# A hybrid streaming encoder layer: state-space and retention products move from GpSimd to VectorE, sampled factors are made first with two load buffers, key weights and the second cache are loaded early

## The chip, the cores and the metric

The kernel runs on one core of one Trainium2 chip. The metric is device time in microseconds of one execution. Five engines work from queues of their own and wait for one another by semaphores: TensorE (PE, whose weight loads are listed as PEld), VectorE (DVE), ScalarE (ACT), GpSimd (POOL) and SyncE (SP). SP computes nothing; it issues nearly all transfers, in the order of its queue.

## The reference

One layer of an encoder on 512 frames of a new stream and on 16 new frames of each of eight running streams: 640 tokens of width 1024. Three mixers read the same normalised projection; their outputs are concatenated and projected back.

```python
def layer(x, pos, ckv_past, krope_past, past_pos, ret_s0, ssm_h0, conv_buf, p):
    x = x + 0.5 * swiglu(rmsnorm(x, p['ffn1_norm']), p['ffn1_wgu'], p['ffn1_wd'])
    cols = rmsnorm(x, p['mix_norm']) @ p['w_in']
    ret_cols, mla_cols, ssm_cols = jnp.split(cols, [RET_COLS, RET_COLS + MLA_COLS], axis=-1)
    o_ret, ret_s = retention_group(...)
    o_mla, c_kv, k_rope = mla_group(...)
    o_ssm, ssm_h, conv_new = ssm_group(...)
    x = x + jnp.concatenate([o_ret, o_mla, o_ssm], axis=-1) @ p['w_out']
    x = x + 0.5 * swiglu(rmsnorm(x, p['ffn2_norm']), p['ffn2_wgu'], p['ffn2_wd'])
```

The running streams bring a cache of 256 latent rows each for the attention (mla_group), and states for retention and for the state-space mixer (ssm_group). The state-space scan, for each chunk and head, is

```python
        xdt = xi * dti[..., None]
        scores = jnp.einsum('bthn,bshn->btsh', ci, bi) * decay
        y = (jnp.einsum('btsh,bshp->bthp', scores, xdt)
             + jnp.einsum('bthn,bhpn->bthp', ci, hs) * jnp.exp(acum)[..., None])
        w = jnp.exp(alast[:, None, :] - acum)
        hs = jnp.exp(alast)[:, :, None, None] * hs + jnp.einsum('bshp,bshn->bhpn', xdt * w[..., None], bi)
```

after which y gets d_skip times x, is gated by silu(z) and normalised.

## The kernel before, in words

Everything is computed in float32. A dense weight or activation is split into a rounded high part and the rest (wh and wl, xh and xl), and each product is three matmuls: high by high, rest by high, high by rest. The high part is an ACT copy (L288), the rest a DVE subtraction (L289). Weights come in pieces of 128x1024 that SP loads.

The stages in the order of time are: FFN1 (to about 450 us), projections for the mixers and attention (450 to 785), convolution and retention (785 to 940), the state-space stage or SSD (940 to 1145), the output projection (to 1190) and FFN2 (to 1628). Code is written in levels of priority (`prio(n)`), and the framework's scheduler orders each engine's queue at build time from these levels and its own estimate of the times; once built, every engine works through a fixed list. So an edit that moves one instruction moves others around it.

What the change touches:

- `spread` (L365) turns a per-token scale into a tile that all partitions hold: two matmuls with a matrix of ones, each copied out of PSUM by ACT (L370). At the start of each FFN, its two halves share one PSUM half (`sb[:, 1]`, L486).
- `wukT`, the key weights of the attention in the latent form, is loaded (L1024) by a transfer that ACT issues just before the matmuls at L1030 use it.
- The sampled attention goes through the eight running streams one by one (`sample_a`, L1140). The cached latents of each are loaded twice, transposed (c_t) and plain (c_n). Stream 0 uses a tile `K` that lies free by then; the others rotate through three buffers.
- The cached rotary keys of all streams (krc) are scaled and rotated by POOL and DVE (L705 to L717).
- Retention multiplies the values by a block mask on POOL (vm, L1370).
- `ssd_a(blk)` (L1530 to L1565) prepares a block of 128 tokens: loads x (yz) and the gate (z), forms xdt = x times dt, xdw = xdt times the decay to the block's end, and yz = x times d_skip, three 128x1024 products on POOL (L1541, L1547, L1548). `ssd_b(blk)` forms the output and the state: yi (L1579) is added to yz on POOL (L1580), the state is scaled and added to on DVE (L1583, L1589), the in-block product on TensorE (L1599) is added (L1600), and the gate is multiplied in (L1601).
- `sample_pre` (L1619 to L1635) makes the factors of the running streams' state update. It loads x of the fifth block into xdw (L1622), scales it on POOL (L1625), splits it (ACT L1628, DVE L1629) and stores the parts to a scratch tensor xw_dr in memory, from which they are read back with the rows of a stream side by side: sr, one load of two transfers for a pair of streams (L1639), with one buffer.
- `sample_step(b)` (L1641) does for stream b and two groups of heads: a load of the state hb, four small matmuls for its output (L1651), hb times the decay on POOL (L1653), the matmul with sr (L1655), the sum on DVE (L1656) and a store.
- `mix_out` (L918) transposes a result into a tile `mo` (two buffers), which SP stores to ma_dr (retention) or ms_dr (SSD). `mix_in` (L1701) loads it back as mraw (three buffers in the first projection) and splits it. `wout` runs the output projection (L1683), first the half with weights woa (retention and attention), whose matmuls also fill the gaps of the SSD stage, then that with weights wos (SSD).
- The gate's projection z (L822) is the other filler; its results are stored through SP to z_dr (L891) and loaded again by `ssd_a` (L1539).

The order of calls is `ssd_a(0)`, `sample_pre()`, and then for each of five blocks: `ssd_a` of the next, two `sample_step`s in each of the first four, `ssd_b`, and `ssd_c` (the transposes) of the one before.

Of the kernel before, what the change touches and what calls it, by code (L numbers as in the profile page):

```python
# [10 lines left out]
F32 = mybir.dt.float32  # L11
# [186 lines left out]
def body(tc, a):  # L198
# [166 lines left out]
    def spread(bank, dg, R):  # L365
        V.tensor_mul(dg.rearrange("p (t c) -> p t c", t=NT), brow(ident, NT), bcol(rstd, P))
        for hf in range(2):
            pr = bank()
            PE.matmul(pr[:, :H2], ones, dg[:, hf * H2:(hf + 1) * H2], start=True, stop=True)
            S.copy(R[:, hf * H2:(hf + 1) * H2], pr[:, :H2])  # L370
# [5 lines left out]
    def xtile(tag, dt=F32):  # L376
        return xt.tile([P, T], dt, tag=tag, name=nm(tag))
# [52 lines left out]
    def ffn(n, tok, first, final, bank, pair, R):  # L430
# [51 lines left out]
        def statistics():  # L482
            with urgent():
                sb = pair()
                norm_stats(lambda: sb[:, 0], G)
                spread(lambda: sb[:, 1], xtile("xl7"), R)  # L486

# [259 lines left out]
    DECB = 5  # L747
    MRAWB = 3
    YZB = 3
# [3 lines left out]
    XWB = 1  # L753
    PRS = 17
    STKB = 1
    SRB = 1
    HBB = 3
# [79 lines left out]
    kf = kvp.tile([P, NC, CR], F32, tag="kf", name="kf")  # L837
    Q.dma_start(out=wukv.rearrange("p a b c -> p (a b c)"), in_=a["wukv"])
    mla_st = ExitStack()
    mp = pool(mla_st, "mlap")  # L840
# [69 lines left out]
    prio(13)  # L910
    spread(one, t0.tile([P, T], F32, tag="sq", name=nm("dg")), R)
    for j, o in ((0, C_QSC), (1, C_KSC)):
# [107 lines left out]
    with ExitStack() as s2:  # L1020
        wk_st = ExitStack()
        wkp = pool(wk_st, "mswk")
        wukT = wkp.tile([64, MH, CKV], F32, tag="wukT", name="wukT")
        nc.scalar.dma_start(out=wukT.rearrange("p h c -> p (h c)"), in_=a["wukT"])  # L1024
        qab = m0.tile([P, 2, DB, MH, DS], F32, tag="qab", name="qab")
# [35 lines left out]
        def prep(u):  # L1061
# [4 lines left out]
            for t in range(4):  # L1066
                pt = one()
                for kv in range(2):
                    for c in range(2):
# [11 lines left out]
                         rs.unsqueeze(3).broadcast_to([P, 4, 4, CR]))  # L1081
            KT = ub.tile([96, 4, SEQ], F32, tag="KT", name=nm("KT"), bufs=2)
            for hh in range(4):
# [51 lines left out]
    with ExitStack() as s2:  # L1135
# [4 lines left out]
        def sample_a(b):  # L1140
            if b == 0:
                kt_ = m0.tile([P, 1600], F32, tag="K", name=nm("K"))
                c_t, c_n = kt_[:, 0:544].rearrange("p (c n) -> p c n", c=2), kt_[:, 544:1056].rearrange("p (c n) -> p c n", c=2)
                iv, krT = kt_[:, 1056:1328], kt_[0:CR, 1328:1600]
            else:
                c_t = t1_.tile([P, 2, 272], F32, tag="c_t", name=nm("c_t"), bufs=3)
                c_n = t1_.tile([P, 2, CKV], F32, tag="c_n", name=nm("c_n"), bufs=3)
                iv = t1_.tile([P, 272], F32, tag="iv", name=nm("iv"))
                krT = t1_.tile([CR, 272], F32, tag="krT", name=nm("krT"))
# [65 lines left out]
    mog_st = ExitStack()  # L1215
    mog = pool(mog_st, "mog", 2)
    ssd_st = ExitStack()
# [115 lines left out]
    def ret_b(blk, rf, vg, qT, at):  # L1333
# [24 lines left out]
        else:  # L1358
            qd = qpad.rearrange("p (b c) -> p b c", c=P + DS)[:, :, 0:DS]
            for r in range(4):  # L1360
# [8 lines left out]
                vm = rb.tile([P, DB, P], F32, tag="vm", name=nm("vm"))  # L1369
                G.tensor_mul(vm, brow(v[:, r * P:(r + 1) * P], DB), bcol(bmask, P))  # L1370
                sc = rb.tile([P, DB, 64], F32, tag="sc", name=nm("sc"))
# [127 lines left out]
    with ExitStack() as s2:  # L1499
# [33 lines left out]
        def ssd_a(blk):  # L1533
# [6 lines left out]
            xdt = big("xdt", XDB)  # L1540
            G.tensor_mul(v16(xdt), v16(yz), bcol(dt[:, blk, :], 64))  # L1541
            bt = xdw = None
            if s == 0:
                bt = sb.tile([P, 256], F32, tag="bt", name=nm("bt"), bufs=BTB)
                trans_b(bt, b0)
                xdw = big("xdw", XWB)
                G.tensor_mul(v16(xdw), v16(xdt), bcol(wl_[:, blk, :], 64))  # L1547
            G.tensor_mul(v16(yz), v16(yz), bcol(rowp[:, R_SSMD:R_SSMD + 16], 64))  # L1548
            pss = bank_a()
# [16 lines left out]
        def ssd_b(blk, bt, xdt, xdw, yz, zt, decs):  # L1566
            s = 1 if blk == 4 else 0
            b0 = blk * P
            for g in range(2):
                gs = slice(g * 512, (g + 1) * 512)  # L1570
                if blk > 0:
# [7 lines left out]
                    V.tensor_mul(v8(yi), v8(pi), bcol(ea[:, blk, 8 * g:8 * g + 8], 64))  # L1579
                    G.tensor_add(yz[:, gs], yz[:, gs], yi)  # L1580
                if s == 0:
# [37 lines left out]
        def sample_pre():  # L1619
            trans_b(bts, SEQ)  # L1620
            xw = big("xdw", XWB)
            Q.dma_start(out=xw, in_=xs_dr[4])  # L1622
            dws = sb.tile([P, SH], F32, tag="dws", name="dws")
            V.tensor_mul(dws, dt[:, 4, :], wl_[:, 4, :])
            G.tensor_mul(v16(xw), v16(xw), bcol(dws, 64))  # L1625
            sh, sl = big("yz", YZB), big("z", ZB)
            bh = sb.tile([P, 256], F32, tag="bh", name="bh")
            S.copy(sh.bitcast(F32R), xw)  # L1628
# [12 lines left out]
        def sample_step(b):  # L1641
# [3 lines left out]
            for g in range(2):  # L1645
# [6 lines left out]
                S.copy(yTs[:, 4 * g:4 * g + 4, b * DS:(b + 1) * DS], pt[:, 0:4 * DS].rearrange("p (c t) -> p c t", c=4))  # L1652
                G.tensor_mul(v8(hb), v8(hb), bcol(els[:, b, 8 * g:8 * g + 8], 64))  # L1653
                pu = bank_s()
                PE.matmul(pu, sr[0][o:o + 48, 1024 + g * P:1024 + (g + 1) * P], sr[0][o:o + 48, gs], start=True, stop=True)  # L1655
                V.tensor_add(hb, hb, pu)  # L1656
                Q.dma_start(out=a["ssms"][b][:, gs], in_=hb)

        cur = ssd_a(0)
        sample_pre()  # L1660
        for blk in range(NT):
            prio(17)
            nxt = ssd_a(blk + 1) if blk + 1 < NT else None
            if blk < 4:
                prio(PRS)
                sample_step(2 * blk)
                sample_step(2 * blk + 1)
                prio(17)
            out = ssd_b(blk, *cur)
# [109 lines left out]
```

## Time and profile before

| | |
|---|---|
| median of 3 runs | 1628.97 us (1628.05 to 1636.07) |
| profiled execution | 1630.27 us, its span 1628.5 us |
| mean granted clock of TensorE | 0.98 |
| TensorE, DVE, ACT, POOL busy | 98%, 69%, 42%, 20% of the span |
| bytes moved | 175.70 MB in 86924 packets |

The span is the time from the first to the last recorded instruction of the profiled execution; the rest of its time lies around it. A line of a group names the source line, the engine, the operation, the tiles (result, then what it reads), the form and the count; then the busy time and the mean of one in ns, and last how long the engine sat idle just ahead and what ended that. A line of the waits says who waited, for which engine's or transfer's result, how long in all, how many times and the longest. In a table by stretches each engine has its busy time (and count of instructions); the granted clock is 1.00 at full speed. The chain is the sequence of work, followed back from the end, in which each step was released by the one before.

### The profile page before, as it was taken

The numbers are of one execution on the slowest core, as the hardware profiler recorded it, in microseconds if no ns is written. First come the engines' busy times: TensorE is split into PE (matmuls) and PEld (weight loads), VectorE is DVE, ScalarE is ACT, GpSimd is POOL, SyncE is SP. The second block draws the span as 40 slices with busy tenths as digits, with TensorE's granted clock in tenths as the row PEclk, the third lists the DMA queues.
The fourth block names the chain that finished last, engine by engine and source line by source line (L and its number), as shares of the span: only waits on it lengthen the run. The fifth ranks groups of instructions, "written<-read, shape, count | busy, mean of one in ns | idle before, by whom it ended". The sixth has DMA issues, their size and how long they took to land.

```text
span 1628.5 us, 27264 instructions
## 1 busy us (share of the span) xinstructions
PE 1592.4 (98%) x10867; PEld 1528.8 (94%) x10867; DVE 1120.2 (69%) x1810; ACT 690.9 (42%) x1270; POOL 332.9 (20%) x361
## 2 busy tenths in 40 slices
PE   9899999999999999999999998999999999999998
PEld 9799999999999999976999887788999999999998
DVE  8878777777575552464799656744779877777762
ACT  7554343334345344553344364423545443433330
POOL 0322222222202000002120134421013222232220
PEclk9999999999999999998999987999999999999999
DMA  5232222222162333213254467764212322222221
GB/s 201 78 104 92 78 78 82 87 78 79 52 205 92 103 111 91 81 53 104 71 180 139 131 188 256 230 188 153 69 46 85 102 80 78 80 90 78 78 78 65
DMA packets 86924, 175.70 MB, mean 108 GB/s; under 512 B 12984, under 2 KB 45144, under 8 KB 86604
## 3 DMA queue, kind: packets, MB, share of 16 engines
q1 hardware_dynamic: 85260, 171.13, 33.2%
q10 hardware_dynamic: 1536, 2.82, 0.6%
q8 instruction: 85, 1.39, 0.4%
q14 instruction: 43, 0.35, 0.1%
HBM read 142.14 MB, written 31.79 MB: 107 GB/s over the span
## 4 chain that ended last, share of the span: by engine, by line
PE 87%; DMA 5%; DVE 4%; ACT 2%; issue 1%; POOL 1%; SPq 0%; ACTq 0%; DVEq 0%; POOLq 0%
PE bank L557 30%; PE pair L600 18%; PE pd L822 11%; PE pd L1683 7%; PE pd L1417 5%; PE pair L464 2%; PE pair L694 1%; PE p L1095 1%; PE po L1117 1%; PE bank L464 1%; PE pb L1599 1%; PE ps L1651 1%; DVE wl L289 1%; DMA xw_dr<-z 1%; DMA sr<-xw_dr 1%
## 5 line engine op out<-in xcount | busy, mean ns | idle before, releaser
L288 ACT CAST wh<-wr 128x1024 fp32r<-128x1024 f32 (+3 forms) x161 | 162.8, 1015 | 174.6 <-PE pair L600 70.7
L289 DVE TENSOR_TENSOR wl<-wr,wh 128x1024 fp32r<-128x1024 f32 (+3 forms) x161 | 198.5, 1234 | 55.6 <-ACT wh L288 50.6
L600 PE MATMUL pair<-xh,wh 128*128 128x320 f32 x672 | 206.6, 309 | 1.1 <-ACT gt L697 0.7
L600 PE MATMUL pair<-xl,wh 128*128 128x320 f32 x672 | 207.4, 309 | 0.0
L600 PE MATMUL pair<-xh,wl 128*128 128x320 f32 x672 | 207.1, 309 | 0.0
L557 PE MATMUL bank<-xsh,wh 128*128 128x320 f32 x656 | 203.0, 310 | 1.6 <-DVE ut L582 1.5
L557 PE MATMUL bank<-xsl,wh 128*128 128x320 f32 x656 | 202.5, 309 | 0.0
L557 PE MATMUL bank<-xsh,wl 128*128 128x320 f32 x656 | 202.5, 309 | 0.0
L524 POOL TENSOR_TENSOR gt<-gt,R 128x320 f32<-128x320 f32 x82 | 93.7, 1143 | 481.5 <-DVE gt L584 427.7
L602 DVE SCALAR_TENSOR_TENSOR x<-pair,x 128x640 f32<-128x640 f32 x96 | 78.7, 822 | 149.9 <-PE pair L600 149.8
L822 PE MATMUL pd<-wh,xh 128*128 128x256 f32 (+1 forms) x560 | 164.2, 293 | 0.1
L822 PE MATMUL pd<-wl,xh 128*128 128x256 f32 (+1 forms) x560 | 163.3, 292 | 0.0
L822 PE MATMUL pd<-wh,xl 128*128 128x256 f32 (+1 forms) x560 | 161.7, 289 | 0.0
L526 POOL TENSOR_TENSOR gt<-gt,R 128x320 f32<-128x320 f32 x82 | 113.8, 1388 | 74.5 <-ACT gt L525 74.5
L600 PEld LDWEIGHTS pair<-xh,wh 128*128 128x128 f32 x672 | 125.8, 188 | 2.1 <-ACT gt L697 1.2
L600 PEld LDWEIGHTS pair<-xl,wh 128*128 128x128 f32 x672 | 126.1, 188 | 0.1
L600 PEld LDWEIGHTS pair<-xh,wl 128*128 128x128 f32 x672 | 126.1, 188 | 0.0
L557 PEld LDWEIGHTS bank<-xsh,wh 128*128 128x128 f32 x656 | 123.3, 188 | 2.9 <-DVE ut L582 2.1
L557 PEld LDWEIGHTS bank<-xsl,wh 128*128 128x128 f32 x656 | 123.3, 188 | 0.3
L557 PEld LDWEIGHTS bank<-xsh,wl 128*128 128x128 f32 x656 | 123.3, 188 | 0.1
L822 PEld LDWEIGHTS pd<-wh,xh 128*128 128x128 f32 x560 | 109.6, 196 | 3.1 <-issue 2.6
L822 PEld LDWEIGHTS pd<-wh,xl 128*128 128x128 f32 x560 | 109.6, 196 | 1.8 <-issue 1.6
(575 smaller groups left out, 4053.9 us busy)
## 6 DMA issues: line engine op xcount, KB each, us to landing
wr<-in_wgu SPq DMA_DIRECT2D x88, 512.0 KB
wr<-in_wd SPq DMA_DIRECT2D x40, 512.0 KB
wr<-in_wint SPq DMA_DIRECT2D x28, 512.0 KB
wr<-in_winx SPq DMA_DIRECT2D x12, 512.0 KB
qk_dr<-stg SPq DMA_DIRECT2D x40, 128.0 KB
wr<-in_woa SPq DMA_DIRECT2D x8, 512.0 KB
hb<-in_sssm SPq DMA_DIRECT2D x16, 256.0 KB
out_ssms<-hb SPq DMA_DIRECT2D x16, 256.0 KB
```

The costliest lines, as they stand in the source:

```text
L288: S.copy(hv, raw)
L289: V.tensor_sub(lv, raw, hv.bitcast(F32))
L464: PE.matmul(out[gu][hf], w_, x_, start=q == 0 and k == 0 and i == 0, stop=q == 3 and k == 1 and i == 2)
L524: G.tensor_mul(gt[:, hf], gt[:, hf], R3[:, hf])
L526: G.tensor_mul(gt[:, hf], gt[:, hf], R3[:, hf])
L557: PE.matmul(out, w_[:, o:o + P], x_[:, PSLOT[p]], start=start and k == 0 and i == 0, stop=k == 3 and i == 2, skip_group_check=not start)
L600: PE.matmul(pt[:, hf, :H2], w_[:, o:o + P], x_[:, hf * H2:(hf + 1) * H2], start=j == 0 and i == 0, stop=j == g - 1 and i == 2)
L602: V.scalar_tensor_tensor(xv, pt[:, :, :H2], 0.5, xv, op0=ALU.mult, op1=ALU.add)
L694: PE.matmul(pt[:, kt], x_[:, o:o + P], w_[cc][:, :512], start=c == 0, stop=c == 5)
L822: PE.matmul(ps[:, :w], x_[k][:, t * P:(t + 1) * P], w_[:, k * w:(k + 1) * w], start=c == 0, stop=c == 23)
L1417: PE.matmul(ps[:, :H2], w_[:, o:o + P], x_[k][:, hf * H2:(hf + 1) * H2], start=c == 0, stop=c == 23)
L1683: PE.matmul(ps[:, :H2], w_[:, o:o + P], x_[k][:, hf * H2:(hf + 1) * H2], start=k == 0 and i == 0, stop=k == NK - 1 and i == 2)
```

## The change

It consists of these edits, all in one diff.

- `spread` takes its two halves from two PSUM halves where it can.
- wukT has a pool of its own, opened at the start of the projections, and is loaded there.
- The tile KT of the first half of the heads is kept in the pool of K; streams 0 and 4 load into K, 1 and 5 into KT, and the other four rotate through two buffers.
- `mo` has one buffer instead of two, mraw two instead of three, sr two instead of one. bh uses a buffer of bt, dws one of qs5.
- The products of `ssd_a`, `ssd_b`, `sample_pre` and `sample_step`, and the masked values vm of retention, are DVE's.
- `sample_pre()` is called ahead of `ssd_a(0)`. The streams of each block are listed in a table, with the same pairs as before.

```diff
@@ spread
-            pr = bank()
+            pr = bank(hf)
...
-                spread(lambda: sb[:, 1], xtile("xl7"), R)
+                spread(lambda hf: sb[:, 1 - hf], xtile("xl7"), R)
...
-    MRAWB = 3
+    MRAWB = 2
...
+    SAMPLED = ((0, 1), (2, 3), (4, 5), (6, 7), ())
...
-    SRB = 1
+    SRB = 2
...
     Q.dma_start(out=wukv.rearrange("p a b c -> p (a b c)"), in_=a["wukv"])
+    wk_st = ExitStack()
+    wkp = pool(wk_st, "mswk", side="right")
+    wukT = wkp.tile([64, MH, CKV], F32, tag="wukT", name="wukT")
+    nc.scalar.dma_start(out=wukT.rearrange("p h c -> p (h c)"), in_=a["wukT"])
...
-            KT = ub.tile([96, 4, SEQ], F32, tag="KT", name=nm("KT"), bufs=2)
+            KT = (ub if u else m0).tile([96, 4, SEQ], F32, tag="KT", name=nm("KT"))
@@ sample_a
-            if b == 0:
-                kt_ = m0.tile([P, 1600], F32, tag="K", name=nm("K"))
+            if b % 4 < 2:
+                kt_ = m0.tile([P, 1600], F32, tag=("K", "KT")[b % 4], name=nm("K"))
...
-                c_t = t1_.tile([P, 2, 272], F32, tag="c_t", name=nm("c_t"), bufs=3)
-                c_n = t1_.tile([P, 2, CKV], F32, tag="c_n", name=nm("c_n"), bufs=3)
+                c_t = t1_.tile([P, 2, 272], F32, tag="c_t", name=nm("c_t"))
+                c_n = t1_.tile([P, 2, CKV], F32, tag="c_n", name=nm("c_n"))
...
-    mog = pool(mog_st, "mog", 2)
+    mog = pool(mog_st, "mog", 1)
...
-                G.tensor_mul(vm, brow(v[:, r * P:(r + 1) * P], DB), bcol(bmask, P))
+                V.tensor_mul(vm, brow(v[:, r * P:(r + 1) * P], DB), bcol(bmask, P))
@@ ssd_a
-            G.tensor_mul(v16(xdt), v16(yz), bcol(dt[:, blk, :], 64))
+            V.tensor_mul(v16(xdt), v16(yz), bcol(dt[:, blk, :], 64))
...
-                G.tensor_mul(v16(xdw), v16(xdt), bcol(wl_[:, blk, :], 64))
-            G.tensor_mul(v16(yz), v16(yz), bcol(rowp[:, R_SSMD:R_SSMD + 16], 64))
+                V.tensor_mul(v16(xdw), v16(xdt), bcol(wl_[:, blk, :], 64))
+            V.tensor_mul(v16(yz), v16(yz), bcol(rowp[:, R_SSMD:R_SSMD + 16], 64))
@@ ssd_b
-                    G.tensor_add(yz[:, gs], yz[:, gs], yi)
+                    V.tensor_add(yz[:, gs], yz[:, gs], yi)
@@ sample_pre
-            dws = sb.tile([P, SH], F32, tag="dws", name="dws")
+            dws = qs5.rearrange("p a t c -> p (a t c)")[:, 0:SH]
...
-            G.tensor_mul(v16(xw), v16(xw), bcol(dws, 64))
+            V.tensor_mul(v16(xw), v16(xw), bcol(dws, 64))
...
-            bh = sb.tile([P, 256], F32, tag="bh", name="bh")
+            bh = sb.tile([P, 256], F32, tag="bt", name="bh", bufs=BTB)
@@ sample_step
-                G.tensor_mul(v8(hb), v8(hb), bcol(els[:, b, 8 * g:8 * g + 8], 64))
+                V.tensor_mul(v8(hb), v8(hb), bcol(els[:, b, 8 * g:8 * g + 8], 64))
@@ the loop over blocks
+        sample_pre()
         cur = ssd_a(0)
-        sample_pre()
...
-            if blk < 4:
-                prio(PRS)
-                sample_step(2 * blk)
-                sample_step(2 * blk + 1)
-                prio(17)
+            prio(PRS)
+            for b in SAMPLED[blk]:
+                sample_step(b)
+            prio(17)
```

How the lists of the engines move is seen at three places. In a row stand the line, the operation, and the tiles written and read; a number behind a name tells tiles of one name apart. The changed file has the same lines up to 5 further down. First SP's queue at the stores of the factors; before:

```order
L1537 DMA yz_10800<-xs_dr_4831 128x1024
L1633 DMA xw_dr<-yz_10785 8x16x1024 x2
L891 DMA z_dr_4820<-stg_10564 128x256
L1539 DMA z_10735<-z_dr_4820 128x1024
L1633 DMA xw_dr<-z_10786 8x16x1024 x2
L1537 DMA yz_10948<-xs_dr_4832 128x1024
L891 DMA z_dr_4821<-stg_10595 128x256
L891 DMA z_dr_4822<-stg_10626 128x256
L1639 DMA sr_10843<-xw_dr 64x1280 x2
L891 DMA z_dr_4823<-stg_10657 128x256
L1539 DMA z_10802<-z_dr_4821 128x1024
```

and after:

```order
L1634 DMA xw_dr<-z_10733 8x16x1024 x2
L896 DMA z_dr_4821<-stg_10419 128x256
L896 DMA z_dr_4822<-stg_10450 128x256
L1705 DMA mraw_11576<-ma_dr 128x320
L896 DMA z_dr_4823<-stg_10481 128x256
L1538 DMA yz_10938<-xs_dr_4832 128x1024
L896 DMA z_dr_4824<-stg_10512 128x256
L1640 DMA sr_10833<-xw_dr 64x1280 x2
L1640 DMA sr_10981<-xw_dr 64x1280 x2
L896 DMA z_dr_4820<-stg_10555 128x256
L896 DMA z_dr_4821<-stg_10586 128x256
L1540 DMA z_10749<-z_dr_4820 128x1024
```

Before, the stores of the factors' low half (read from a z tile) come behind a store and a load of the gate (z_dr, z), and the first load of sr behind two more stores; one load of sr stands there. After, both pairs of sr are loaded ahead of the last two gate stores, and the gate loads of the first blocks follow them.

Then TensorE's queue around the first matmul with sr, before:

```order
L822 MATMUL pd_10662<-wl_10535,xh_644_4767 128x256
L1585 MATMUL pb_11061<-xdw_10811,bt_10806 128x512
L822 MATMUL pd_10662<-wh_10534,xh_653_4788 128x256
L822 MATMUL pd_10662<-wh_10534,xl_654_4789 128x256
L822 MATMUL pd_10662<-wl_10535,xh_653_4788 128x256
L1683 MATMUL pd_11648<-xh_1965_11580,wh_11638 128x320
L1683 MATMUL pd_11648<-xl_1966_11581,wh_11638 128x320
L1683 MATMUL pd_11648<-xh_1965_11580,wl_11639 128x320
L1655 MATMUL ps_10855<-sr_10843 128x512
L1651 MATMUL ps_10861<-bc,hb_10859 128x16 x4
L1599 MATMUL pb_11066<-xdt_10804,dec_10821 128x64 x4
```

and after:

```order
L823 MATMUL pd_10591<-wl_10520,xh_651_4784 128x256
L823 MATMUL pd_10591<-wh_10519,xh_635_4743 128x256
L1575 MATMUL pb_11036<-state_10720,bc 128x512
L1531 MATMUL pa_10945<-ident,bc 128x128 x2
L1656 MATMUL ps_10845<-sr_10833 128x512
L1652 MATMUL ps_10851<-bc,hb_10849 128x16 x4
L823 MATMUL pd_10591<-wh_10519,xl_636_4744 128x256
L823 MATMUL pd_10591<-wl_10520,xh_635_4743 128x256
L823 MATMUL pd_10591<-wh_10525,xh_638_4751 128x256
L823 MATMUL pd_10591<-wh_10525,xl_639_4752 128x256
L823 MATMUL pd_10591<-wl_10526,xh_638_4751 128x256
```

Before, the gate's projection (L822) is at its end when the first L1655 comes, and after it there follow matmuls of the SSD stage and of the output projection (L1683). After, the first L1656 stands among rows of the gate's projection (now L823), of which 62 follow it.

Last DVE's queue in the first block, before:

```order
L890 SCALAR_TENSOR_TENSOR stg_10564<-jnk_10563,stg_10564 128x256
L1579 TENSOR_TENSOR yi_11048<-pb_11046,E 128x512
L1583 TENSOR_TENSOR state_10729<-state_10729,E 128x512
L1562 TENSOR_TENSOR dec_10833<-dec_10833,stm_10817 128x512
L1562 TENSOR_TENSOR dec_10839<-dec_10839,stm_10817 128x512
L1629 TENSOR_TENSOR z_10786<-xdw_10780,yz_10785 128x1024
L890 SCALAR_TENSOR_TENSOR stg_10595<-jnk_10594,stg_10595 128x256
L1553 TENSOR_TENSOR stm_10965<-pa_10962,cst 128x256
L1601 TENSOR_TENSOR yz_10733<-yz_10733,z_10735 128x512 x2
```

and after:

```order
L1580 TENSOR_TENSOR yi_11038<-pb_11036,E 128x512
L1584 TENSOR_TENSOR state_10720<-state_10720,E 128x512
L1549 TENSOR_TENSOR yz_10938<-yz_10938,rowp 128x1024
L1657 TENSOR_TENSOR hb_10836<-hb_10836,ps_10845 128x512
L1654 TENSOR_TENSOR hb_10849<-hb_10849,E 128x512
L1581 TENSOR_TENSOR yz_10790<-yz_10790,yi_11038 128x512
L1554 TENSOR_TENSOR stm_10955<-pa_10952,cst 128x256
L1602 TENSOR_TENSOR yz_10747<-yz_10747,z_10749 128x512 x2
L1590 TENSOR_TENSOR state_10720<-state_10720,pb_11042 128x512
L1580 TENSOR_TENSOR yi_11047<-pb_11045,E 128x512
```

Before, the block's DVE work is decay (L1562), sums and the split of the factors (L1629). After, the POOL products stand among it (L1549, L1654, L1581), the split is gone from this place, and the product with the gate (L1602, which reads z) stands ahead of the state's sum (L1590).

More of the change, by code (lines that the diff above doesn't have):

```diff
@@ L910, in body @@
     prio(13)
-    spread(one, t0.tile([P, T], F32, tag="sq", name=nm("dg")), R)
+    spread(lambda hf: one(), t0.tile([P, T], F32, tag="sq", name=nm("dg")), R)
     for j, o in ((0, C_QSC), (1, C_KSC)):
@@ L1020, in body @@
     with ExitStack() as s2:
[L1021 to L1024, printed above, removed]
         qab = m0.tile([P, 2, DB, MH, DS], F32, tag="qab", name="qab")
```

## The prediction

> **What bounds the kernel now.** I read the page first: busy times, granted clock, the chain.
>
> ```profile
> span 1628.5 us, 27264 instructions
> PE 1592.4 (98%) x10867; PEld 1528.8 (94%) x10867; DVE 1120.2 (69%) x1810; ACT 690.9 (42%) x1270; POOL 332.9 (20%) x361
> PEclk9999999999999999998999987999999999999999
> PE 87%; DMA 5%; DVE 4%; ACT 2%; issue 1%; POOL 1%; SPq 0%; ACTq 0%; DVEq 0%; POOLq 0%
> ```
>
> TensorE sets the time, and nothing in the change takes a matmul of any size away. What can be won is the rest: places where TensorE waits, and the half clock that follows them. A slice of the clock row is 40.7 us; it dips in the 19th (733 to 774 us) and the 24th and 25th (936 to 1018). The next view is the list of TensorE's waits between 440 and 1220 us, where all edits but one lie (us in total, times, longest).
>
> ```profile
> PE ps L1655 <- DMA sr<-xw_dr: 7.0, 2, 4.4
> PE pd L1683 <- ACT xh L1710: 2.1, 2, 1.5
> PE pd L1683 <- DVE xl L1711: 2.1, 2, 1.4
> PE p L1163 <- DMA c_t<-in_ckvT: 1.7, 1, 1.7
> PE px L1030 <- DMA wukT<-in_wukT: 1.4, 1, 1.4
> PE pb L1585 <- DVE state L1589: 0.8, 1, 0.8
> ```
>
> Then a table by stretches; after the busy times of PE, PEld, DVE, ACT and POOL comes the granted clock, then the DMA share.
>
> ```profile
> 600.00:640.00 40.00, 38.58 (x286) 36.84 (x286) 8.05 (x23) 16.40 (x46) 0.52 (x2) 0.91 0.36 99
> 720.00:780.00 60.00, 54.75 (x333) 42.29 (x331) 28.34 (x80) 22.54 (x76) 8.47 (x45) 0.91 0.27 79
> 890.00:940.00 50.00, 49.69 (x390) 45.44 (x389) 34.74 (x92) 20.93 (x40) 7.59 (x4) 1.00 0.50 142
> 940.00:960.00 20.00, 18.77 (x145) 17.28 (x143) 9.05 (x11) 15.07 (x29) 4.93 (x3) 0.96 0.65 200
> 960.00:980.00 20.00, 20.00 (x89) 14.84 (x90) 14.11 (x16) 9.42 (x18) 10.84 (x6) 0.67 0.57 171
> 980.00:1000.00 20.00, 16.26 (x99) 13.27 (x98) 12.80 (x29) 9.34 (x20) 5.33 (x4) 0.93 0.62 178
> 1000.00:1020.00 20.00, 19.34 (x83) 16.89 (x84) 13.06 (x20) 8.72 (x20) 8.51 (x5) 0.59 0.87 324
> 1020.00:1060.00 40.00, 37.83 (x213) 29.60 (x213) 32.17 (x59) 16.25 (x32) 19.45 (x12) 0.96 0.71 234
> 1088.00:1110.00 22.00, 19.42 (x111) 17.65 (x109) 5.54 (x8) 2.85 (x6) 4.18 (x4) 0.84 0.42 130
> 1110.00:1150.00 40.00, 36.53 (x242) 34.61 (x242) 22.60 (x48) 16.35 (x30) 2.56 (x2) 0.96 0.48 151
> ```
>
> A busy TensorE at a clock of 0.67 loses a third of the stretch, and no wait shows it: 20 x 0.33 = 6.6 us in 960 to 980, 20 x 0.41 = 8.2 us in 1000 to 1020. Last the chain of waits through the state-space (SSD) stage, start and length first.
>
> ```profile
> 965.77 5.50 DMA xdw<-xs_dr
> 971.43 1.91 POOL xdw L1625
> 975.70 2.01 DVE stg L890
> 977.73 6.57 DMA z_dr<-stg
> 985.38 10.93 DMA xw_dr<-z
> 996.37 4.25 DMA sr<-xw_dr
> 1089.30 5.38 DMA sr<-xw_dr
> 1133.24 5.48 DMA mraw<-ms_dr
> ```
>
> The first sampled product waits for a train of transfers that begins only at 965.77; SP issues the store of the factors' low half at 985.38, after the z store of 977.73 that stands ahead of it in the queue. The second sr is loaded at 1089.30, because one buffer serves all eight streams.
>
> **Key weights.** The load of wukT moves from just before its use (issued by ACT, TensorE waiting 1.4 us) to the start of the projections. The half clock that follows goes too: 40 x (1 - 0.91) = 3.6 us in 600 to 640, a stretch with no other wait of size. That makes 1.4 + 3.6 = 5.0, and 1.4 if the clock falls anyway.
>
> ```profile
> L1030 PE MATMUL px<-qTs,wukT x32: 271/272/579, 619.7 to 628.9; 64*128 64x128 f32 x32
> ```
>
> The same matmul takes 272 ns or 579 ns within one wait's reach, so a wait of 1.4 us was followed by half speed. [...]
>
> The pools shift as well, and the cached rotary keys are prepared some 35 us earlier: their load and their first POOL product now stand ahead of the last gate product of FFN1.
>
> ```profile
> L710 POOL TENSOR_TENSOR kg_c<-krc x1: 1041/1041/1041, 485.0 to 485.0; 128x512 f32<-128x512 f32 x1
> ```
>
> That product costs FFN1's end between nothing and its 1.0 us plus the load's lateness; with the half clock of the wukT row I bound it by 5, and take 1.
>
> **Sample caches.** Two samples of each four read into buffers that lie free, so their loads run during attention. The 1.7 us at c_t goes; of the 60 x 0.09 = 5.4 us of clock in 720 to 780 some, because several short waits remain. Bounds 0 and 7; I take 3, since the chain from scores to values is as it was.
>
> **First sr.** The load at 965.77 moves ahead of every block's work, and SP reaches the stores of the factors behind weights and not behind z. Their splitting runs on DVE, ACT, DVE without POOL. By the rows above, store and load take 10.9 + 4.3 = 15.2 us; with the stores issued around 961 (DVE frees the last weights by about 959, as now) sr lands near 977. TensorE comes to its first use at about 978, and by the order 62 dense z rows still follow as filler where before none was left. So 4.4 us of wait go, and with them the 8.2 us of clock in 1000 to 1020: 12.6. The clock of 960 to 980 stays, since the dependent chain at the block's start stays. Back comes a wait: the stores and loads of z now stand behind sr on SP. 6.57 us for a z store and 5.5 us for a load of that size from about 974 put z at 986; the gate product that waits for it stands ahead of the next state sum on DVE, and TensorE would want that sum at about 981. I take 5 us, net 12.6 - 5 = 7.6. Bounds: -4 (the wait stays at 4.4 + 4 in another place) and 16 (z no later than needed, and half of the 6.6 us regained).
>
> **Second sr.** With two buffers the load of 1089.30 is issued an early pair ahead. In 1088 to 1110 TensorE idles 22 - 19.42 = 2.6 us and loses 22 x 0.16 = 3.5 us of clock: 6.1, at least 2.6.
>
> **The tail.** The last transposes of y now stand 103 output-projection matmuls ahead of the first that needs them, where 12 stood.
>
> ```profile
> 1128.08 0.31 PE L1683 MATMUL pd<-xh,wl 128*128 128x320 f32 x1
> ...
> 1129.39 0.31 PE L1683 MATMUL pd<-xh,wl 128*128 128x320 f32 x1
> 1131.21 0.57 PE L1683 MATMUL pd<-xh,wh 128*128 128x320 f32 x2 [1.50 <-ACT xh L1710]
> ```
>
> From the first to the second of these rows nine matmuls start in 1.31 us, 146 ns each, so the cover grows from 1.8 to 15 us. The way it must hide runs from the transposes at 1127 to the last xl near 1141, 14 us; the single transpose buffer adds about one store of some 3 us to it (an estimate from half of the 5.48 us load), but the last chunks are used later still. Idle 40 - 36.53 = 3.5 and clock 40 x 0.04 = 1.6 us give 5.1; bounds 2 and 7. The third load buffer that the mixer loses belongs to loads that are far ahead, cost 0, and if that cover is gone one load's 5.48 us in part. The decay vector and the split of b that take another tile's place cost 0: each is read once, ahead of the tile's next owner.
>
> **POOL's products on DVE.** Their rows, and what DVE takes for the like:
>
> ```profile
> L1653 POOL TENSOR_TENSOR hb<-hb,E 128x512 f32<-128x512 f32 x16 | 18.9, 1178 | 54.9 <-PE ps L1651 51.5 <-DVE x L1728 3.4
> L1580 POOL TENSOR_TENSOR yz<-yz,yi 128x512 f32<-128x512 f32 x8 | 11.6, 1446 | 19.1 <-DVE yi L1579 19.0
> L1548 POOL TENSOR_TENSOR yz<-yz,rowp 128x1024 f32<-128x1024 f32 x5 | 10.9, 2174 | 0.2
> L1600 DVE TENSOR_TENSOR yz<-pb,yz 128x512 f32<-128x512 f32 x10 | 6.9, 688 | 9.8 <-PE pb L1599 9.8
> L1629 DVE TENSOR_TENSOR z<-xdw,yz 128x1024 fp32r<-128x1024 f32 x1 | 1.2, 1212 | 0.0
> L289 DVE TENSOR_TENSOR wl<-wr,wh 128x1024 fp32r<-128x1024 f32 x13 | 20.8, 1609 | 5.0 <-ACT wh L288 4.8
> L267 DVE TENSOR_TENSOR rst<-rsy 128x2 f32<-128x2 f32 x15 | 6.2, 416 | 0.3
> ```
>
> 24 half-width products at 0.69 us and 15 full-width ones at 1.21 us are 16.6 + 18.2 = 34.8 us more for DVE between 940 and 1130; four more (vm, 4.8 us) fall in 890 to 940, where DVE has 15 us free and TensorE is not kept waiting. Against that, DVE's own work shortens: the weight split takes 1609 ns here against the 1212 ns of the same shape, 13 x 0.4 = 5.2 us, and a step on two columns takes 416 ns. Each product alone is also quicker, 0.69 for 1.18 to 1.45 us. DVE has 120 - 81.2 = 38.8 us idle between 940 and 1060 (the five rows of the table), so the work fits; but it is a queue, and a product waiting for POOL's old input now holds up what follows. The state waits (0.8 us, and xl's 1.4 in 1020 to 1060) gain up to 3.8 us with their clock (2.2 idle, 1.6 clock), the new order may lose 8; I take a loss of 2.
>
> The second half of the sum of squares in another bank lets the second spreading matmul go ahead of the first copy, at the two FFN starts. One copy less in a chain of several is worth up to 1 us; I cost it at 0.
>
> **Sum.** 5.0 - 1 + 3 + 7.6 + 6.1 + 5.1 - 2 = 23.8 us. The profiled execution took 1630.3 us (span 1628.5 and 1.8 around it), 1.3 above the median of the three runs, 1629.0; so 1606.5 for it, and for the median **1605.2 us**.
>
> **Rivals.**
> *DVE's queue holds half of it.* Between blocks TensorE, ACT and DVE hand one another each step, and sr's wait may be only the last that such a train ends in: then its 12.6 us are not won, and half of the added 34.8 us lies on the path. What is left is the gains outside, 5.0 - 1 + 3 + 6.1 + 5.1 = 18.2, less 17.4: 0.8 us, 1628.2. For it: DVE is busy 32.17 of 40 us in 1020 to 1060, and its new order ties z, state and split together. Against: DVE holds 4% of the chain, and sr's train of transfers starts with a load that nothing of DVE holds back.
> *DVE becomes the bound, slower.* The same, but DVE's 38.8 us of idle time are all such handing over, so that all 34.8 us lengthen the stage: 34.8 - 18.2 = 16.6 us slower, 1645.6. It decides from 18.2 + 8.1 = 26.3 us on the path, three quarters of the added work. Against: much of DVE's idle time waits for TensorE itself (9.8 us before L1600), and POOL, which took longer for the same products, holds 1% of the chain.
> *The clock doesn't come back.* If the short waits that remain keep the clock low, its terms fall: 3.6 for wukT, 2 of the samples' 3, half of sr's 8.2, 3.5 and 1.6, together 14.8; 23.8 - 14.8 = 9.0 are left, 1620.0. The row of L1030 speaks against, and the 1.00 of 890 to 940, where no wait of size stands, speaks for a clock that recovers. [...]
> *More comes.* z is in time and the clock holds from 960 on: 7.6 becomes 16, samples 7, and the loss of 2 goes: 1591.
>
> **How the numbers follow.** Forecast (1597 to 1614) 0.55; more 0.13; clock lost 0.12; half on DVE's queue 0.11; slower 0.09. About 0.5%, 8.1 us, is what a measurement of this kernel can tell from no change, so below 1620.9 counts as faster: the first two and half of the third, 0.74. Within 0.5%: the other half and the fourth, 0.17. Slower: 0.09. The range leaves out the slow rival, the half of the fourth that lies above 1628 and what of "more" lies below 1588, some 0.2 together: 1588 to 1628.
>
> **What would show it.** Right: no wait of px on wukT and L1030 at 272 ns throughout; the sr rows at most 1.5 us of wait in all; a clock over 0.9 in the 20 us after the first sampled product; no ACT or DVE wait at the first matmuls of the second output projection; DVE's weight split near 1.2 us in the SSD stage. Wrong in a term: TensorE waiting for state or yi on DVE for over 5 us, DVE waiting for z. Wrong as a whole: DVE's share of the chain rising from 4% to 6% or more while the stage of 940 to 1150 keeps its 210 us.

## The result, and the profile after

The changed kernel takes 1606.5 us (median of 4 executions, 1604.7 to 1607.7), the kernel before 1629.2: a ratio of 0.985, 95% interval 0.982 to 0.988, 22.8 us faster. The forecast was 1605.2. The profiled execution has a span of 1605.9 us. Its page, in the lines that answer to those shown of before:

```profile
span 1605.9 us, 27198 instructions
PE 1572.9 (98%) x10867; PEld 1515.4 (94%) x10867; DVE 1127.4 (70%) x1853; ACT 693.4 (43%) x1270; POOL 264.8 (16%) x318
PEclk9999999999999999999999988899999999999999
PE 49%; DMA 3%; DVE 1%; ACT 0%; POOL 0%; issue 0%; SPq 0%; DVEq 0%; ACTq 0%; POOLq 0%
```

POOL has lost 43 instructions and 68 us, DVE has gained the 43 and only 7 us. (The chain covers about half of the span this time, so its shares can't be held against those of before.) TensorE's waits between 440 and 1220 us in the changed kernel:

```profile
PE pd L1683 <- ACT xh L1710: 6.8, 2, 6.4
PE ps L1652 <- DMA hb<-in_sssm: 2.6, 1, 2.6
PE pair L600 <- DVE al L381: 2.4, 1, 2.4
PE pa L1559 <- ACT dec L1561: 1.4, 2, 0.7
PE pair L600 <- ACT ah L380: 0.5, 1, 0.5
```

The waits for sr, for wukT, for c_t and for the state are gone. New are one of 6.4 us at the output projection's first operands, one of 2.6 us for the first loaded state, and 2.9 us at the end of FFN1. The table by stretches (busy times of PE, PEld, DVE, ACT, POOL, then clock, DMA share, GB/s):

```profile
600.00:640.00 40.00, 40.00 (x323) 38.49 (x323) 12.43 (x30) 19.37 (x49) 0.53 (x2) 1.00 0.28 89
720.00:780.00 60.00, 55.60 (x372) 44.84 (x372) 31.44 (x95) 22.60 (x74) 8.85 (x46) 1.00 0.24 73
940.00:960.00 20.00, 16.03 (x94) 13.73 (x94) 12.54 (x16) 14.64 (x25) 0.00 (x0) 0.80 0.73 241
960.00:980.00 20.00, 19.27 (x100) 15.04 (x99) 12.49 (x18) 6.58 (x13) 0.00 (x0) 0.76 0.74 226
980.00:1000.00 20.00, 20.00 (x123) 16.02 (x123) 16.42 (x32) 10.57 (x22) 0.00 (x0) 0.93 0.57 190
1000.00:1020.00 20.00, 13.40 (x72) 10.48 (x72) 13.14 (x40) 10.04 (x22) 0.00 (x0) 0.83 1.04 346
1020.00:1060.00 40.00, 39.65 (x227) 32.30 (x226) 34.54 (x64) 15.52 (x30) 0.00 (x0) 0.96 0.75 253
1060.00:1090.00 30.00, 30.00 (x219) 28.32 (x218) 19.23 (x40) 9.78 (x21) 0.00 (x0) 1.00 0.37 124
1090.00:1150.00 60.00, 60.00 (x414) 59.88 (x413) 38.48 (x76) 28.32 (x47) 0.00 (x0) 1.00 0.42 132
```

From 1060 to 1150 us TensorE neither waits nor slows; before, the two stretches after 1088 lost 11 us there. The clock in 600 to 640 and 720 to 780 is full. Between 940 and 1020 TensorE still loses both ways.

Every execution, not only the profiled one, comes with its span and mean clock. Span x (1 - clock) is the time for which the clock was lost (half clock while TensorE idles is counted too: in the changed kernel no matmul starts from 1009.95 to 1013.40 us, at a clock of 0.50), and the rest of the span is an estimate of what the same execution would take at full clock, as far as TensorE sets the time. Medians for the kernel before (47 executions, run beside the experiments): 27.7 lost and 1598.6 of rest; for the changed kernel (4 executions) 12.8 and 1591.7. So about 15 us of the gain are clock and 7 us the rest, waits above all. All experiments are read in these two numbers, as medians of 4 to 11 executions; the clock is given to a thousandth, 1.6 us. The lost time of one execution spreads widely (17.8 to 44.3 us among the 47, 9.6 to 16.1 among the 4), so differences of a few us between two variants say little.

### The profile page after: what moved, and what is told of

It reads as the page before. It is cut to its first block, busy times and chain, and to the rows that moved or that the text cites. A ratio compares the mean times of both kernels' runs of the same rounds, so it can differ in the third digit from the quotient of the medians.

```text
span 1605.9 us, 27198 instructions
## 1 busy us (share of the span) xinstructions
PE 1572.9 (98%) x10867; PEld 1515.4 (94%) x10867; DVE 1127.4 (70%) x1853; ACT 693.4 (43%) x1270; POOL 264.8 (16%) x318
## 4 chain that ended last, share of the span: by engine, by line
PE 49%; DMA 3%; DVE 1%; ACT 0%; POOL 0%; issue 0%; SPq 0%; DVEq 0%; ACTq 0%; POOLq 0%
PE bank L557 15%; PE pair L600 10%; PE pd L1683 7%; PE pd L1418 5%; PE pd L823 3%; DMA z_dr<-stg 1%; PE pb L1600 1%; PE pair L464 1%; DMA mraw<-ma_dr 1%; PE ps L1652 1%; DMA hb<-in_sssm 0%; DMA sr<-xw_dr 0%; PE pb L1366 0%; PE pb L1377 0%; PE pb L1343 0%; PE pb L927 0%
## 5 line engine op out<-in xcount | busy, mean ns | idle before, releaser
L289 DVE TENSOR_TENSOR wl<-wr,wh 128x1024 fp32r<-128x1024 f32 (+3 forms) x161 | 193.2, 1203 | 66.9 <-ACT wh L288 62.2
L823 PE MATMUL pd<-wh,xh 128*128 128x256 f32 (+1 forms) x560 | 162.4, 290 | 0.7 <-ACT stg L894 0.7
L823 PE MATMUL pd<-wl,xh 128*128 128x256 f32 (+1 forms) x560 | 162.5, 290 | 0.0
L823 PE MATMUL pd<-wh,xl 128*128 128x256 f32 (+1 forms) x560 | 161.5, 288 | 0.0
L823 PEld LDWEIGHTS pd<-wh,xh 128*128 128x128 f32 x560 | 108.6, 194 | 3.6 <-issue 1.9
L823 PEld LDWEIGHTS pd<-wl,xh 128*128 128x128 f32 x560 | 108.5, 194 | 2.4 <-issue 2.2
```

The source lines that it names most:

```text
L289: V.tensor_sub(lv, raw, hv.bitcast(F32))
L823: PE.matmul(ps[:, :w], x_[k][:, t * P:(t + 1) * P], w_[:, k * w:(k + 1) * w], start=c == 0, stop=c == 23)
```

## The experiments

**1. The moved products alone.** The kernel before with this edit at all seven places where the change makes it (vm, xdt, xdw, yz, yi's sum, xw, hb), and no other:

```diff
-            G.tensor_mul(v16(xdt), v16(yz), bcol(dt[:, blk, :], 64))
+            V.tensor_mul(v16(xdt), v16(yz), bcol(dt[:, blk, :], 64))
...
```

> The kernel before with one part of the change alone: the state-space products, the sampled products and the masked values go from GpSimd to VectorE, nothing else. My theory (the moved products lie beside other work, a loss of about 2 us): 1625 to 1634 us, with the two waits for sr still there. Rival one (VectorE's queue becomes the bound): 1640 us or more, TensorE waiting for VectorE between the blocks. Rival two (the quicker products are where the gain of the change comes from): 1615 us or less.

Measured: 1612.5 us, ratio 0.990 (0.988 to 0.992); lost 20.9, rest 1590.9. That is in rival two's range, and the step of the prediction that counted a loss of 2 us is refuted in its sign. The trace tells where. The chain of the kernel before, just ahead of the load with which the factors begin at 965.77:

```profile
960.74 2.92 DVE wl L289
963.65 1.53 DVE stg L890 x2
965.28 0.38 SPq L891
```

and that of this run up to the first product with sr:

```profile
953.65 1.14 DVE wl L289
956.99 1.15 DVE xdw L1625
966.65 1.14 DVE z L1629
968.44 10.42 DMA xw_dr<-z
978.92 4.08 DMA sr<-xw_dr
```

Before, a weight split that takes 2.92 us beside POOL's products holds up the gate's staging, whose store stands on SP's queue ahead of the factors' load. SP also waited for two such splits, until 960.8 and 963.7, since the weight loads ahead of the factors' load need the tiles that they free (its waits from 940 to 975 us):

```profile
SPq L297 <- DVE wl L289: 7.0, 2, 4.6
```

Now the split takes 1.14 us and SP waits for none. But SP's list differs, too: in run 1 the factors' load, issued at 952.85, stands ahead of these two weight loads and not behind them, so the quicker steps and the new order aren't told apart here. sr is loaded at 978.92 instead of 996.37, though the factors are made in the same place of the program; 7.7 us of that lead this execution had already at the end of retention, by lost clock that it was spared, and 9.7 us are the stage's own, 5.2 of them won by the time the factors' load is issued. TensorE also comes earlier and still waits for it:

```profile
PE ps L1655 <- DMA sr<-xw_dr: 4.2, 1, 4.2
```

So the products pay beyond sr: with one sr buffer there is no second wait, and 1.6 us are left of the tail's.

**2. The changed kernel with all products back on POOL**, the reverse edit:

```diff
-            V.tensor_mul(v16(xdt), v16(yz), bcol(dt[:, blk, :], 64))
+            G.tensor_mul(v16(xdt), v16(yz), bcol(dt[:, blk, :], 64))
...
```

> The changed kernel with only the products put back on GpSimd. My theory: within 5 us of the changed kernel, 1602 to 1612 us, since what VectorE takes over it gets back in steps that GpSimd no longer stretches. Rival one (the products on VectorE cost what the rest won): 1595 us or less. Rival two (they are the gain): 1620 us or more.

Measured: 1617.4 us, 0.993 (0.991 to 0.995) of before; lost 28.3, rest 1588.4. Neither 5 us nor 14: the products are worth 10.9 us here, and all of it is clock, since the rest is even 3 us shorter than in the changed kernel. The other edits together, without the products, win 11.8 us; the two shares add to 28.5 where both give 22.8.

**3 and 4. The third load buffer.** A third mraw buffer doesn't fit beside two sr, so a control makes room first.

```diff
-    DECB = 5
+    DECB = 4
@@ in run 4 also
-    MRAWB = 2
+    MRAWB = 3
```

> A control for the next one: the changed kernel with four instead of five buffers for the decay tiles, which frees 2 KB a partition. All theories: within 3 us of the changed kernel, 1603 to 1610 us, with the wait of about 6.4 us for the output projection's first operands still there.

> The control with three load buffers for the output projection's operands, as before the change, instead of two. My theory now (the one big wait left in the changed kernel, 6.4 us at 1007 us, comes from the missing third buffer, a cost that I had put at 0): the wait and the 3.4 us of clock behind it go, 1594 to 1600 us. Rival (it comes from SP's queue, in which the loads stand behind those of sr, whatever the buffers): the wait stays, 1603 to 1610 us.

Measured: 1608.8 us (lost 19.3, rest 1587.7) and 1612.8 us (lost 25.0, rest 1586.0). The control hadn't the wait of 6.4 us at all, since its order is another, and was no faster for that. In run 4 a wait for xh is there,

```profile
PE pd L1683 <- ACT xh L1710: 2.5, 1, 2.5
```

and the time is no better than the control's, above the range of either theory. My explanation of the 6.4 us by the missing buffer predicted 1594 to 1600 and is wrong as a price: the rest is 5.7 us below that of the changed kernel, and the lost clock 12.2 us above it.

**5. The sampled factors first, alone.** In the kernel before:

```diff
+        sample_pre()
         cur = ssd_a(0)
-        sample_pre()
```

> The kernel before with one part alone: the sampled factors are made ahead of the first block's preparation; products on GpSimd, one buffer for sr. After the first four runs I have two theories of where the gain sits. Theory A (both the moved products and the early factors pay by the same thing, sr landing before TensorE reaches it; either is enough): sr's first wait goes here too and the time is 1615 to 1622 us. Theory B (the gain is the products' own speed, wherever the factors are made): no more than 4 us here, 1625 to 1630 us.

Measured: 1631.8 us, 1.000 (0.997 to 1.002); lost 37.5, rest 1592.8. The time lies above both ranges, nearer to theory B's. Theory A is refuted in its price: TensorE doesn't wait for sr any more and the rest falls by 5.8 us, but the lost clock rises by 9.8. The waits that come are for the states,

```profile
PE pb L1599 <- DVE state L1589: 3.5, 2, 2.5
PE pd L1683 <- DVE x L1728: 2.9, 1, 2.9
PE ps L1655 <- DVE hb L1656: 2.6, 1, 2.6
```

and two stretches of its profiled execution (1621.9 us, the shortest of its eleven) show the clock:

```profile
980.00:1000.00 20.00, 16.75 (x83) 14.11 (x82) 16.07 (x38) 10.08 (x25) 6.91 (x5) 0.66 0.42 122
1020.00:1060.00 40.00, 39.03 (x178) 32.46 (x177) 26.41 (x54) 17.26 (x35) 11.84 (x8) 0.68 0.60 195
```

TensorE is busy 39 of 40 us in the second and runs at two thirds: a chain of small steps, without waits that a list would show.

**6. The key weights early, alone.** In the kernel before:

```diff
     Q.dma_start(out=wukv.rearrange("p a b c -> p (a b c)"), in_=a["wukv"])
+    wk_st = ExitStack()
+    wkp = pool(wk_st, "mswk", side="right")
...
-        wk_st = ExitStack()
-        wkp = pool(wk_st, "mswk")
...
```

> The kernel before with one part alone: the key weights in a pool of their own, loaded at the start of the projections (the early preparation of the rotary keys comes with it). By the forecast's terms 5.0 won and 1 lost: 1625 us, 1623 to 1627. Rival (what is won at the weights is lost at the end of the first FFN, and the clock falls elsewhere): 1628 to 1631 us.

Measured: 1631.5 us, 1.001 (0.998 to 1.003); lost 29.3, rest 1599.3. The rival comes nearest; its range ends half a microsecond lower. The wait for wukT (1.4 us) is gone and this one has come:

```profile
PE pair L600 <- DVE al L381: 2.4, 1, 2.4
```

**7 and 8. Which products.** The changed kernel with only hb (L1654) back on POOL, and with only the 128x1024 ones (xdt, xdw, yz, xw):

```diff
@@ run 7
-                V.tensor_mul(v8(hb), v8(hb), bcol(els[:, b, 8 * g:8 * g + 8], 64))
+                G.tensor_mul(v8(hb), v8(hb), bcol(els[:, b, 8 * g:8 * g + 8], 64))
@@ run 8
-            V.tensor_mul(v16(xdt), v16(yz), bcol(dt[:, blk, :], 64))
+            G.tensor_mul(v16(xdt), v16(yz), bcol(dt[:, blk, :], 64))
...
```

> The changed kernel with only the sixteen decay products of the running streams' states (hb) back on GpSimd. VectorE waited 10.1 us for them in the run with all products on GpSimd. If these are what costs there: 1612 to 1618 us. If the block products are: 1604 to 1609 us.

> The changed kernel with only the 128x1024 products of the blocks and of the sampled factors (xdt, xdw, yz, xw) back on GpSimd. If these are what costs with all products on GpSimd, since they stand in the chain of each block's start: 1611 to 1617 us, most of it as time at half clock between 950 and 1060 us. If the hb products are: 1604 to 1609 us.

Measured: 1613.5 us (lost 22.6, rest 1588.8) and 1619.9 us (lost 30.8, rest 1589.3). Both cost, the large ones 13.4 us (2.9 above the range expected) and hb 7.0 (within it). Putting back the large ones alone doesn't cost clearly more than putting back all (10.9 in run 2): both runs have a ratio of 0.993 to the kernel before, run beside them. Again it is clock; the rest is 2 to 3 us below that of the changed kernel. Prices of parts don't add here.

**9. The large products alone** on DVE, in the kernel before:

```diff
-            G.tensor_mul(v16(xdt), v16(yz), bcol(dt[:, blk, :], 64))
+            V.tensor_mul(v16(xdt), v16(yz), bcol(dt[:, blk, :], 64))
...
```

> The kernel before with only the 128x1024 products (xdt, xdw, yz of the blocks, xw of the sampled factors) on VectorE; the others stay on GpSimd. All products moved took the kernel before from 1629 to 1612.5 us, and these put back took the changed kernel to 1620. Theory (it is these, because each block starts with them and the sampled factors wait for their tile): 1614 to 1620 us. Rival (it is the small products, or only all together): 1624 to 1631 us.

Measured: 1613.4 us, 0.991 (0.987 to 0.995); lost 24.2, rest 1587.4. That is just under the theory's range: these fifteen instructions bring what all 43 bring in that kernel. The first sr is loaded at 982.1 instead of 996.4, but TensorE, which comes earlier too, still waits 6.1 us for it.

**10. One sr buffer** in the changed kernel.

```diff
-    SRB = 2
+    SRB = 1
```

> The changed kernel with one buffer for sr instead of two. By the forecast's term (2.6 us of wait and 3.5 us of clock at the second and later loads): 1609 to 1614 us. Rival (in the run with the products moved alone there was one buffer and no wait for a later sr, so the second buffer is worth nothing): 1604 to 1608 us.

Measured: 1607.6 us; lost 16.1, rest 1589.4. The rival holds: the second buffer is worth nothing that shows. Its order has other waits in place of the 6.4 us:

```profile
PE ps L1652 <- DMA hb<-in_sssm: 7.7, 3, 4.4
```

**11. The factors second** in the changed kernel:

```diff
-        sample_pre()
         cur = ssd_a(0)
+        sample_pre()
```

> The changed kernel with the sampled factors made after the first block's preparation, as before the change. By the forecast's term for the first sr: 1612 to 1617 us. Rival (the early factors alone left the kernel before at 1632 us, so they are worth nothing by themselves, and with the quick products the load comes early anyway): 1603 to 1609 us.

Measured: 1628.9 us, 1.000 (0.998 to 1.002); lost 37.4, rest 1590.3. Both expectations missed. Without this edit the change brings nothing, and with it alone (run 5) neither; the rest is 8 us better than before and all is given back in clock:

```profile
980.00:1000.00 20.00, 11.61 (x38) 7.72 (x37) 12.36 (x21) 4.46 (x10) 0.00 (x0) 0.58 0.90 247
1000.00:1020.00 20.00, 17.46 (x58) 12.50 (x56) 12.60 (x40) 9.34 (x19) 0.00 (x0) 0.57 1.04 383
1020.00:1060.00 40.00, 38.70 (x144) 28.48 (x145) 27.29 (x50) 9.63 (x23) 0.00 (x0) 0.62 0.44 138
```

In 1020 to 1060 TensorE starts 144 matmuls where the changed kernel starts 227, at 0.62 against 0.96, and is listed as busy for nearly the same time. The slow time begins at 983 us, with a wait of TensorE of 5.9 us for the state. DVE's list there (start, length) shows where that wait comes from:

```profile
986.54 1.23 DVE L1542 TENSOR_TENSOR xdt<-yz,dt 128x1024 f32<-128x1024 f32 x1 [5.29 <-DMA yz<-xs_dr]
987.68 0.68 DVE L1590 TENSOR_TENSOR state<-state,pb 128x512 f32<-128x512 f32 x1
```

The next block's product, now in DVE's queue, waits 5.3 us for its load, and the state's sum stands behind it. In the kernel before, POOL waited 25.1 us for such a load ahead of its product at 954.99, with no state sum in its queue. This is the price of the move that the forecast feared, in an order in which the load comes late.

**12. A try for more.** The changed kernel with the key weights' pool opened behind the preparation of the rotary keys.

```diff
     Q.dma_start(out=wukv.rearrange("p a b c -> p (a b c)"), in_=a["wukv"])
-    wk_st = ExitStack()
...
     cache_keys()
+    wk_st = ExitStack()
+    wkp = pool(wk_st, "mswk", side="right")
...
```

> A try for a faster one: the changed kernel with the key weights' pool opened behind the preparation of the rotary keys, so that this preparation goes back to where it was and the load still comes 100 us early. The waits of 0.5 and 2.4 us at the end of the first FFN go: 1602 to 1605 us, if the order of the state-space stage, which moves with it, is no worse; 1606 to 1612 us if the clock there falls more often.

Measured: 1615.7 us, above both ranges; lost 29.1, rest 1585.1. The waits at FFN1's end went and the rest is the shortest of all, 6.6 us below that of the changed kernel; the clock took 16 us. No version here beats the changed kernel.

## Why the prediction was right, and where only its sum was

The sum was right, 23.8 us forecast and 22.8 measured, and so was its split: the clock terms, as the third rival adds them up, came to 14.8 us and the lost clock fell by 14.9; 9.0 were left for the waits and the rest fell by 6.9. The places were mostly not those where I put them, and that the sum came out so close is luck: a term of the wrong sign and terms worth nothing made up for each other. The profiled executions show it. At the end of retention the changed kernel is 7.9 us ahead, where the terms for key weights and samples make 7.0; but run 1, which has none of these edits, is 7.8 us ahead there, because the profiled kernel before had lost 8.5 us of clock on the way that run 1 didn't lose. From there to the first matmul of FFN2 the change wins 14.5 us, where the other terms make 16.8; run 1 wins 11.6 of them with the products alone.

- *Key weights, 5.0 less 1.* In the two profiled executions the stretch from the first gate matmul to the last with wukT is 5.5 us shorter and FFN1 ends 3.3 us later. The clock at these matmuls was 1.00, 272 ns is their median, and none took over 373 ns, where one took 579 before:

```profile
L1031 PE MATMUL px<-qTs,wukT x32: 272/272/373, 620.9 to 627.1; 64*128 64x128 f32 x32
```

 The early keys cost 2.9 us of wait, for which I took 1. Alone the edit gains nothing (run 6). The 3.6 us of clock didn't come in every execution: run 1 waits 1.1 us at the same matmuls, and its rows from 980 to 1090 us hold 22.1 of the 22.5 us of clock that its profiled execution lost.
- *Samples, 3.* The profiled executions give 5.0 us from the end of attention to the last of the sampled attention. Run 1, without this edit, gives 4.5 over the same stretch, by no loss of clock. The edit's own part is some 0.5 us.
- *First sr, 7.6.* The mechanism came out: I had sr landing near 977 and its first use at 978. TensorE uses it first at 977.4 and doesn't wait for it. That it fits to the microsecond is partly luck: SP issued the factors' last stores at 952 to 957, not at 961, and the load 14 us behind the last one, at 970.5.

```profile
977.43 0.72 PE ps L1656
...
999.21 7.21 DMA sr<-xw_dr
1006.48 6.57 DMA mraw<-ma_dr
1014.78 5.54 DMA mraw<-ma_dr
```

 In the 20 us from there the clock is 0.87, where over 0.9 was to show the term right. The new wait came too, but at another place: not at the state behind the late gate (DVE waited 1.0 us for z), but at the output projection, whose operands were loaded behind the third pair of sr. The price fails alone (run 5: 0) and is far too small in company (run 11: 22 us).
- *Second sr, 6.1.* Refuted by run 10; run 1 also has one buffer and no such wait.
- *Spreading, third load buffer, 0.* The first is right: the wait of 1.5 us before L369 stands in both kernels. The second I can't call: its load set the 6.4 us wait, but with it back the time is no better (run 4).
- *Tail, 5.1.* No wait and a full clock after 1060 us, as forecast. Run 1 keeps 1.6 us of wait there without the new place of the transposes, so most of the waiting goes without that part of the change.
- *Products, -2.* Wrong in sign. What was right is the arithmetic of DVE, by the groups of the changed kernel between 930 and 1120 us:

```profile
L289 DVE TENSOR_TENSOR wl<-wr,wh 128x1024 fp32r<-128x1024 f32 x14 | 16.9, 1220 | 5.9 <-ACT wh L288 5.9
L1654 DVE TENSOR_TENSOR hb<-hb,E 128x512 f32<-128x512 f32 x16 | 11.0, 686 | 5.0 <-PE ps L1652 5.0
L1542 DVE TENSOR_TENSOR xdt<-yz,dt 128x1024 f32<-128x1024 f32 x5 | 6.1, 1221 | 0.9 <-DMA yz<-xs_dr 0.9
L267 DVE TENSOR_TENSOR rst<-rsy 128x2 f32<-128x2 f32 x15 | 2.3, 156 | 0.3
```

 0.69 and 1.22 us per product and 1220 instead of 1609 ns for the split are as written. The step that failed is that I booked the stretched steps as DVE's busy time only. They stand ahead of loads and stores on SP's queue and of TensorE's next operands, and with them moves a train of transfers that TensorE waits for: by 9.7 us in run 1, of which that one split is 1.8 and the new order of SP's list a part that isn't measured. Two readings failed with it: that DVE frees the last weights by about 959, and that nothing of DVE holds back the load with which sr's train starts. SP's 7.0 us of wait for the splits, until 963.7, stood ahead of that load.
- *The rivals.* DVE as the bound is out: it gained 7 us of work in the whole kernel, and run 1 was faster. Its mechanism exists all the same, a product that waits at the head of DVE's queue (run 11). That the clock doesn't come back is what happened in runs 5 and 11.

Shown are the totals, the shares of clock and rest, and that both the products and the early factors are needed with the other edits (runs 2, 8, 11). Not settled is why just the changed kernel's order keeps the clock, which is two thirds of the gain: each variant gets another order of all engines from the scheduler, so none is a clean subtraction, and the lost clock follows the order.

## What to carry to other kernels

Split each execution into span x (1 - clock) and the rest before a gain is explained; where a stage hands work between engines in small steps, removed waits can come back as half clock (run 5: the rest 5.8 us shorter, the lost clock 9.8 us longer), and an edit's price alone says little of its price in company. Clock losses of one profiled execution are one draw (17.8 to 44.3 us among 47 executions of the kernel before): before booking them as a saving, see whether they stand in other executions too. Work that stretches another engine's steps (a weight split of 2.92 us beside POOL's products, of 1.14 us in run 1) is priced where the stretched steps are waited for, at the head of queues, not by busy time.

## What the runs showed of the hardware

*The same waits cost clock in one execution and none in another.* The wait of 2.4 us at the end of FFN1, and one of 0.5 us just ahead of it, stand in the changed kernel and in run 2 alike. The stretch around them, first in the changed kernel, then in run 2 (clock behind the busy times of the five engines):

```profile
445.00:465.00 20.00, 16.92 (x112) 16.13 (x111) 15.80 (x26) 6.38 (x9) 5.53 (x7) 1.00 0.47 143
```

```profile
445.00:465.00 20.00, 17.09 (x96) 16.56 (x95) 15.56 (x25) 6.00 (x8) 5.17 (x6) 0.83 0.44 140
```

In the first no clock is lost, in the second 20 x 0.17 = 3.4 us. So the length of the waits alone doesn't settle what they cost; what does isn't shown.

*The clock fell for 3.4 to 17.1 us at a time.* In the profiles of the two kernels, between 440 and 1220 us, the clock was 0.50 in such a stretch and 1.00 between them. The kernel before has eight stretches, the shortest from 1030.18 to 1033.59 us, the longest from 999.46 to 1016.52, beginning within the wait of 4.4 us for sr; the changed kernel has four, the longest of 10.2 us. In run 11 some 64 of the 80 us from 980 to 1060 were at half clock (an estimate: twice the 32.2 us that its three rows above lose), though TensorE is listed as busy for 67.8 of them. That a chain of small steps keeps the clock down is my reading of its 240 matmuls there against 422 in the changed kernel; half clock itself makes part of that difference.

*Small matmuls fill little.* At full clock the sampled output's matmuls of 16 columns and the in-block ones of 64 mostly start 111 to 112 ns apart, those of 128 columns 108 to 112. As an estimate I gave a column 0.84 ns (a matmul of 512 columns that isn't part of a split product mostly starts about 429 ns ahead of the next): by it, those of 16 and 64 columns leave almost nine tenths and half of that time empty. Of the 63 matmuls in the longest half-clock stretch of the kernel before, 48 are of these two kinds.
